# Sums of a normalised input taken from PSUM, tile by tile, in a one-core Trainium2 transformer layer

## The chip, the cores and the metric

The kernel is one program on one core of one Trainium2 chip. The core has a matrix engine (TensorE, called PE in the profile, with its weight loads as PEld), a vector engine (VectorE, DVE), an activation engine (ScalarE, ACT), a general engine (GpSimd, POOL) and a queue that issues the DMA transfers (SyncE, SP). Each engine works through its own list of instructions in order, and waits for the others through semaphores. The metric is the device time of one execution in microseconds (us).

## The reference, cut to what matters

One decoder layer on 1024 tokens of width 1024, in float32. What the change touches is its second half: the residual sum, the second norm, and the feed-forward (FF) block of width 2816.

```python
h = x + merged @ w_out
hn = rms_norm(h, norm_ffn)
return h + (jax.nn.silu(hn @ w_gate) * (hn @ w_up)) @ w_down
```

Every float32 operand is held as a high part (rounded to the matrix engine's type) and a low part (what is left over), and every product is three matmuls: high by high, high by low, low by high.

## The kernel before, in words

**The output projection and the norm.** The 1024 tokens are four tiles of 256 rows, `tp` = 0 to 3. The loop over `c4` computes 256 columns of `h` at a time: `tok_proj` (48 matmuls of 256 columns) for each tile, an add of `x` on VectorE, and the squares on ScalarE. In the last round (`c4` = 3) `norm_h` follows one tile behind. It multiplies the tile's rows by their reciprocal norm and by the gain (`scalar_tensor_tensor`, two of 1024 elements), turns them with 16 transposes into four PSUM banks, and for each bank takes the high half on ScalarE and the low half on VectorE (`split`, 512 elements each) into the operand slabs `XN[half]`. Here `half` is the left or right operand of 512 tokens: tiles 0 and 1 are half 0, tiles 2 and 3 half 1. The program has eight PSUM banks: seven for `bank` in three small pools, one for `fbank`.

**FF blocks the plain way.** FF has 22 blocks of 128 columns. `plain(f, half, w)` is the direct way: 24 matmuls of 512 columns for the gate, 24 for the up projection, `silu` on ScalarE, the product on VectorE. Block 0 is done so after the last output projection, with tile 3's norm between its halves, and so is block 1. One block takes 96 matmuls.

**FF blocks with seven products.** From block 2 on `seven` computes the four products of half by gate or up with the Winograd form of Strassen's scheme: seven products of half the depth, 12 matmuls each, 84 in all. It wants sums of the weights, which `pieces` makes one block ahead (four operations on GpSimd, splits on ScalarE and VectorE), and four sums of the normalised input, `T[0]` to `T[3]`, each in two slabs (`j` = 0, 1). `sums` makes these after the norm from the slabs `XN`, high and low parts apart: `j` = 0 on GpSimd and `j` = 1 on VectorE, ten operations of 1024 elements each, and then splits them. Block 1 stands behind `sums` in program order.

**What sets the order.** The program is written in the order above; a scheduler then places the instructions on each engine by priority and by when their operands and buffers are free. Buffers come from pools that are reused in turn: 16 slabs, 4 of 4 KB per partition (`t4`), 6 of 2 KB (`t2`), 2 of `fz`, 2 staging buffers for weights. A slab that held `h` of a tile can be reused only when that tile has been stored to memory (`hd`), because `h` is wanted again at the end.

Of the kernel before, what the change touches and what calls it, by code (L numbers as in the profile page):

```python
# [8 lines left out]
F32 = mybir.dt.float32  # L9
# [3 lines left out]
OP = mybir.AluOpType  # L13
# [25 lines left out]
def hybrid_layer_kernel(  # L39
# [26 lines left out]
    def nm(s):  # L66
        count[0] += 1
        return f"{s}_{count[0]}"

    def slab(shape, dt=F32R):  # L70
        return slabs.tile([P] + shape, dt, tag="slab", name=nm("slab"))
# [13 lines left out]
    def t4(shape, dt=F32):  # L85
        return t4p.tile([P] + shape, dt, tag="t4", name=nm("t4"))
# [39 lines left out]
    def sub(eng, o, a, b):  # L126
        eng.tensor_tensor(o, a, b, op=OP.subtract)  # L127

    def split(hi, lo, src, eng=None):
        nc.scalar.copy(hi, src)  # L130
        sub(eng or nc.vector, lo, src, hi.bitcast(F32))
# [70 lines left out]
    def transpose_pair(js, dests):  # L202
        for kp in range(4):
            b = bank([2, 256])
            for kk in range(2):
                k = 2 * kp + kk
                for tt in range(2):
                    nc.tensor.transpose(b[:, kk, tt * P:(tt + 1) * P], js[tt][:, k * P:(k + 1) * P], ident)  # L208
            hi, lo = dests(kp)
            split(hi, lo, b)  # L210
# [605 lines left out]
    def left_low(f, a0, a1):  # L816

        s_ = t2([512])
        sub(nc.gpsimd, s_, a0, a1)
        nc.sync.dma_start(ads[2, f], s_)  # L820
# [14 lines left out]
    def gate_up(f):  # L835
        return [col_unit(w, f * P, alloc=anyslab) for w in (w_gate, w_up)]

    def plain(f, half, w):
# [5 lines left out]
        emit_act(f, half, s_)  # L844
        return s_

    def norm_h(tp):
        half, q = tp // 2, tp % 2
        if q == 0:
            for kp in range(4):  # L850
                XN[half][kp] = slab([2, 2, 512])
        ss = small(2)
        nc.vector.tensor_reduce(ss, sq4[tp].rearrange("p (t c) -> p t c", t=2), axis=AX.X, op=OP.add)
        r = recip_rms(ss, D, RMS_EPS, 2)
        js = (t4([D]), t4([D]))
        for tt in range(2):
            nc.vector.scalar_tensor_tensor(js[tt], H[tp][:, tt, :], r[:, tt:tt + 1], gff, op0=OP.mult, op1=OP.mult)
        transpose_pair(js, lambda kp: tuple(XN[half][kp][:, hl, :, q * 256:(q + 1) * 256] for hl in range(2)))

    H = [None] * 4  # L860
    gff = fstp.tile([P, D], F32, tag="fst", name="gff")
# [2 lines left out]
    for c4 in range(4):  # L864
        ws = row_units(w_out, c4 * 256, alloc=anyslab)
        if c4 == 3:
            w0 = gate_up(0)
        for tp in range(4):
            xr = t2([2, 256])
            nc.sync.dma_start(xr, x[tp * 256:(tp + 1) * 256, c4 * 256:(c4 + 1) * 256]  # L870
                              .rearrange("(t p) d -> p t d", p=P))
            if c4 == 0:
                H[tp] = slab([2, D], F32)
            ps = tok_proj(ws, tp, mg, anybank)
            h = H[tp][:, :, c4 * 256:(c4 + 1) * 256]
            nc.vector.tensor_tensor(h, ps, xr, op=OP.add)
            for tt in range(2):
                nc.scalar.activation(xr[:, tt], h[:, tt], AF.Square, accum_out=sq4[tp][:, 4 * tt + c4:4 * tt + c4 + 1])
            if c4 == 3 and tp > 0:
                norm_h(tp - 1)  # L880
    a0 = plain(0, 0, w0)
    norm_h(3)
    left_low(0, a0, plain(0, 1, w0))


    T = [[None] * 2 for _ in range(4)]

    def sums(j, eng):
        def add(o, a_, b_):
            eng.tensor_tensor(o, a_, b_, op=OP.add)  # L890

        (l0, l1), (r0, r1) = [[XN[h_][j + 2 * u][:].bitcast(F32) for u in range(2)] for h_ in range(2)]
        d = []
        for n_ in range(4):
            v = t4([2, 512])
            if n_ in (0, 2):
                p_, q_ = (r0, l0) if n_ == 0 else (r1, r0)
                e = t4([2, 512])
                sub(eng, v, p_[:, 0], q_[:, 0])
                sub(eng, e, p_[:, 1], q_[:, 1])  # L900
                add(v, v, e)
            else:
                p_, q_ = (r1, d[0]) if n_ == 1 else (l1, d[1])
                sub(eng, v, p_[:, 0], q_)
                add(v, v, p_[:, 1])
            d.append(v)
            T[n_][j] = slab([2, 2, 512])
            split(T[n_][j][:, 0], T[n_][j][:, 1], v)

    def pieces(f):  # L910
        st = []
# [59 lines left out]
        emit_act(f, 0, c11)  # L971
        (left_low if f < FH else left_high)(f, c11, u4)

    for tp in range(4):
        nc.sync.dma_start(hd[tp], H[tp])
    sums(0, nc.gpsimd)
    sums(1, nc.vector)
    w1 = gate_up(1)
    left_low(1, plain(1, 0, w1), plain(1, 1, w1))
    w = pieces(2)  # L980
    for f in range(2, FF // P):
        nxt = pieces(f + 1) if f + 1 < FF // P else None
        seven(f, *w)
        w = nxt
# [92 lines left out]

    def into(B, th, dh, final):
        for t in range(4):
            h = H[2 * th + t // 2][:, t % 2, cols[dh]]  # L1080
            nc.vector.tensor_tensor(h, B[t], h, op=OP.add)
            if final:
                r0 = th * 512 + t * P
                nc.sync.dma_start(out[r0:r0 + P, cols[dh]], h)

    product(X, p1, True)
# [42 lines left out]
```

## Time and profile before

| what | value |
|---|---|
| time, median of 3 runs | 1765.89 us (1764.24 to 1766.59) |
| time of the profiled execution | 1765.17 us |
| its span, first to last instruction | 1763.4 us |
| mean granted TensorE clock | 0.991 |
| PE busy | 1706.7 us, 97% of the span |
| DVE, ACT, POOL busy | 1071.1, 724.7, 664.4 us |
| chain that ended last | PE 84%, DVE 10%, POOL 2% of the span |

The chain that ended last is followed back from the last instruction, at each step to what released it. Nearly all of it is PE; where another engine stands in it, PE waited there.

### The profile page before, as it was taken

How to read it: one execution, taken by the hardware profiler on the slowest of the kernel's cores; microseconds unless marked ns; L12 is line 12 of the kernel's file. 1: busy time of each engine (PE TensorE's matmuls, PEld its weight loads, DVE VectorE, ACT ScalarE, POOL GpSimd, SP SyncE). 2: the span in 40 equal slices, each digit the busy share in tenths (PEclk: the TensorE clock that was granted, in tenths of full speed). 3: DMA queues.
4: the chain of work that ended last, by engine and by line, in shares of the span. 5: the costliest groups of instructions: out<-in, count | busy, mean ns of one | idle time of the engine just before them, and what ended most of it. 6: DMA issues, size and time to landing. Idle time of an engine off the chain costs nothing.

```text
span 1763.4 us, 25092 instructions
## 1 busy us (share of the span) xinstructions
PE 1706.7 (97%) x9431; PEld 1482.2 (84%) x9431; DVE 1071.1 (61%) x1794; ACT 724.7 (41%) x1355; POOL 664.4 (38%) x543
## 2 busy tenths in 40 slices
PE   7999779999999999999999999989999999999999
PEld 6887669899988888989888899868888888888887
DVE  5599994435445667767755623596454554457655
ACT  6212224344455666766654423333222222234332
POOL 1113458333343434434203500456656767510000
PEclk9999899999999999999999999989999999999999
DMA  6113314211122111111286323123233444794673
GB/s 220 48 27 114 126 42 132 78 55 39 65 66 64 49 37 49 37 34 46 86 300 202 121 73 120 72 72 120 90 107 117 140 156 157 245 394 166 213 242 124
DMA packets 178527, 204.59 MB, mean 116 GB/s; under 512 B 10788, under 2 KB 125764, under 8 KB 177382
## 3 DMA queue, kind: packets, MB, share of 16 engines
q1 hardware_dynamic: 178406, 202.99, 35.2%
q8 instruction: 74, 1.21, 0.3%
q14 instruction: 47, 0.39, 0.1%
HBM read 152.62 MB, written 50.33 MB: 115 GB/s over the span
## 4 chain that ended last, share of the span: by engine, by line
PE 84%; DVE 10%; POOL 2%; ACT 1%; DMA 1%; issue 1%; SPq 0%; DVEq 0%; ACTq 0%; POOLq 0%
PE ps L141 51%; PE pf L141 16%; PE ps L1064 11%; DVE slab L360 6%; PE ps L714 3%; PE pf L1064 1%; DVE slab L127 1%; POOL wsl L127 1%; DVE t L127 1%; POOL t L127 1%; PE ps L208 1%; DMA slab<-in_x_dram 1%; DMA fst<-in_w_in_dram 0%; PE ps L640 0%; PE ps L515 0%
## 5 line engine op out<-in xcount | busy, mean ns | idle before, releaser
L141 PE MATMUL ps<-slab,wsl 128*128 128x512 f32 x1596 | 370.9, 390 | 0.3 <-ACT wsl L130 0.3
L141 PEld LDWEIGHTS ps<-slab,wsl 128*128 128x128 f32 x1596 | 299.0, 188 | 63.1 <-ACT wsl L130 0.8
L141 PE MATMUL pf<-slab,fsl 128*128 128x512 f32 x1260 | 327.8, 399 | 4.5 <-ACT fz L765 1.8
L141 PEld LDWEIGHTS pf<-slab,fsl 128*128 128x128 f32 x1260 | 226.6, 188 | 46.8 <-ACT fz L765 3.6
L141 PE MATMUL ps<-wsl,slab 128*128 128x256 f32 x1744 | 235.7, 291 | 12.9 <-POOL wsl L127 8.1
L141 PEld LDWEIGHTS ps<-wsl,slab 128*128 128x128 f32 x1744 | 225.3, 198 | 16.7 <-POOL wsl L127 8.5
L360 DVE SCALAR_TENSOR_TENSOR slab<-slab,cw 128x1007 f32<-128x1007 f32 (+27 forms) x120 | 174.5, 1501 | 0.4
L954 DVE TENSOR_TENSOR t<-ps,t 128x512 f32<-128x512 f32 x124 | 85.0, 688 | 109.2 <-PE ps L141 104.4
L127 DVE TENSOR_TENSOR t<-ps,t 128x512 fp32r<-128x512 f32 (+2 forms) x192 | 117.5, 630 | 44.6 <-ACT t L130 43.1
L141 PE MATMUL ps<-slab,fsl 128*128 128x512 f32 x612 | 142.1, 389 | 0.0
L141 PEld LDWEIGHTS ps<-slab,fsl 128*128 128x128 f32 x612 | 114.9, 188 | 23.9
L1064 PE MATMUL ps<-wsl 128*128 128x512 f32 x504 | 120.6, 389 | 0.0
L127 POOL TENSOR_TENSOR wsl<-st,wsl 128x1024 fp32r<-128x1024 f32 x20 | 72.9, 3659 | 122.9 <-ACT wsl L130 110.4
L141 PE MATMUL ps<-t,slab 128*128 128x256 f32 x624 | 115.6, 292 | 2.6 <-DVE t L127 2.1
L130 ACT CAST t<-ps 128x512 fp32r<-128x512 f32 (+2 forms) x192 | 97.9, 540 | 42.1 <-PE ps L714 30.5
L130 ACT CAST wsl<-st 128x1024 fp32r<-128x1024 f32 x66 | 69.3, 1050 | 110.5 <-PE ps L141 66.4
L1064 PEld LDWEIGHTS ps<-wsl 128*128 128x128 f32 x504 | 94.6, 188 | 19.6
L141 PEld LDWEIGHTS ps<-t,slab 128*128 128x128 f32 x624 | 93.9, 189 | 9.5 <-DVE t L127 3.0
L141 PE MATMUL ps<-slab,qt 128*128 128x384 f32 (+3 forms) x384 | 96.2, 342 | 0.5 <-DVE sm L682 0.5
L127 POOL TENSOR_TENSOR fsl<-fst,fsl 128x1024 fp32r<-128x1024 f32 x24 | 62.7, 2614 | 81.2 <-ACT fsl L130 81.2
L127 DVE TENSOR_TENSOR wsl<-st,wsl 128x1024 fp32r<-128x1024 f32 x46 | 62.3, 1355 | 49.9 <-ACT wsl L130 49.8
L628 POOL TENSOR_SCALAR wsl<-wsl,sm 128x640 f32<-128x640 f32 (+7 forms) x76 | 52.7, 707 | 91.2 <-DVE sm L626 53.4
(238 smaller groups left out, 2772.5 us busy)
## 6 DMA issues: line engine op xcount, KB each, us to landing
t<-in_w_down_dram SPq DMA_DIRECT2D x70, 256.0 KB, 3.8
fst<-in_w_in_dram SPq DMA_DIRECT2D x24, 512.0 KB, 3.9
zd<-fz SPq DMA_DIRECT2D x48, 256.0 KB, 2.0
t<-zd SPq DMA_DIRECT2D x24, 512.0 KB, 3.5
st<-in_w_in_dram SPq DMA_DIRECT2D x22, 512.0 KB, 3.9
st<-in_w_gate_dram SPq DMA_DIRECT2D x22, 512.0 KB, 4.0
st<-in_w_up_dram SPq DMA_DIRECT2D x22, 512.0 KB, 4.4
ad<-t SPq DMA_DIRECT2D x44, 256.0 KB, 2.4
```

The lines of the kernel that those rows point to most:

```text
L127: eng.tensor_tensor(o, a, b, op=OP.subtract)
L130: nc.scalar.copy(hi, src)
L141: return nc.tensor.matmul(o, a, b, start=start, stop=stop)
L208: nc.tensor.transpose(b[:, kk, tt * P:(tt + 1) * P], js[tt][:, k * P:(k + 1) * P], ident)
L360: nc.vector.scalar_tensor_tensor(acc[:, s:], u[:, :S - s], cw[:, ct, 30 - s:31 - s], acc[:, s:], op0=OP.mult, op1=OP.add)
L628: nc.gpsimd.tensor_scalar(tiles[h], tiles[h], c[:, h:h + 1], 1.0, op0=OP.mult, op1=OP.mult)
L714: nc.tensor.transpose(b[:, j - j0, h, :], tiles[h][:, j * P:(j + 1) * P], ident)
L954: nc.vector.tensor_tensor(o, a_, b_, op=OP.add)
L1064: nc.tensor.matmul(B[t], a_, b_, start=start and k == 0 and j == 0, stop=k == FH - 1 and j == 2, skip_group_check=True)
```

## The change

Tiles 0 and 2 are now half 0 and tiles 1 and 3 half 1, so that a pair of tiles (0 and 1, then 2 and 3) gives 256 columns of both halves. `norm_h` of an even tile copies the four turned banks, besides splitting them, to SBUF (`raw`). `norm_h` of an odd tile subtracts: its own banks in PSUM against `raw` give the sums for those 256 columns, eight operations of 512 elements on VectorE, and `keep` splits each of them into its half of the slab `T[n][j]`. Of the first pair, the splits of `T[1]` and `T[2]` are put off until the last output projection has been written, those of `T[3]` until the second pair. The function `sums` is gone, with its twenty operations of 1024 elements, GpSimd's ten among them. Block 1 is done by `seven`, and `pieces(1)` takes the place of `gate_up(1)`. The stores of `h` are issued per tile. The rows of the output are addressed by the new halves.

```diff
     def norm_h(tp):
-        half, q = tp // 2, tp % 2
+        half, q = tp % 2, tp // 2
+        c = slice(q * 256, (q + 1) * 256)
...
-        transpose_pair(js, lambda kp: tuple(XN[half][kp][:, hl, :, q * 256:(q + 1) * 256] for hl in range(2)))
+        def turned(kp):
+            b = bank([2, 256])
+            for kk in range(2):
+                k = 2 * kp + kk
+                for tt in range(2):
+                    nc.tensor.transpose(b[:, kk, tt * P:(tt + 1) * P], js[tt][:, k * P:(k + 1) * P], ident)
+            split(XN[half][kp][:, 0, :, c], XN[half][kp][:, 1, :, c], b)
+            return b
+
+        def keep(n, j, v, c=c):
+            if T[n][j] is None:
+                T[n][j] = slab([2, 2, 512])
+            split(T[n][j][:, 0, :, c], T[n][j][:, 1, :, c], v)
+
+        if half == 0:
+            raw[0], raw[1] = [sb_fz() for _ in range(2)], t4([2, 2, 256])
+            for kp in range(4):
+                nc.scalar.copy(raw[0][kp] if kp < 2 else raw[1][:, kp - 2], turned(kp))
+            return
+        for j in range(2):
+            r0, r1 = turned(j), turned(j + 2)
+            l0, l1 = raw[0][j], raw[1][:, j]
+            d0, d1, d2 = (t2([2, 256]) for _ in range(3))
+            sub(nc.vector, d0, r0, l0)
+            keep(0, j, d0)
+            sub(nc.vector, d1, r1, d0)
+            sub(nc.vector, d2, d1, l0)
+            sub(nc.vector, l1, l1, d1)
+            later = [lambda n=n, j=j, v=v: keep(n, j, v) for n, v in ((1, d1), (2, d2))]
+            held[0] += later
+            held[1].append(lambda j=j, v=l1: keep(3, j, v))
+            if q == 1:
+                for f_ in held[0] + held[1][j::2]:
+                    f_()
+                held[0].clear()
...
-            if c4 == 3 and tp > 0:
-                norm_h(tp - 1)
+            if c4 == 3:
+                nc.sync.dma_start(hd[tp], H[tp])
+                if tp == 3:
+                    for f_ in held[0]:
+                        f_()
+                    held[0].clear()
+                if tp > 0:
+                    norm_h(tp - 1)
...
-    sums(0, nc.gpsimd)
-    sums(1, nc.vector)
-    w1 = gate_up(1)
-    left_low(1, plain(1, 0, w1), plain(1, 1, w1))
-    w = pieces(2)
-    for f in range(2, FF // P):
+    w = pieces(1)
+    for f in range(1, FF // P):
```

**VectorE around the add of tile 3.** This is VectorE's list around the last add of the output projection, which writes tile 3's columns into `slab_10303`; before, with the end of tile 2's norm ahead of it and the start of tile 3's norm (`TENSOR_REDUCE`) behind it:

```order
L857 SCALAR_TENSOR_TENSOR t_1885_11134<-slab_10248,sm_11132,gff 128x1024
L857 SCALAR_TENSOR_TENSOR t_1886_11135<-slab_10248,sm_11132,gff 128x1024
L127 TENSOR_TENSOR wsl_11382<-st_11380,wsl_11382 128x1024
L876 TENSOR_TENSOR slab_10303<-ps_11072,t_1876_11070 128x2x256
L853 TENSOR_REDUCE sm_11220<-sm_10125 128x2
```

Now, where `slab_10938` to `slab_10940` are the low halves of tile 2 and the other slabs ahead of the add are parts of `T`:

```order
L127 TENSOR_TENSOR slab_10938<-ps_11184,slab_10938 128x2x256
L127 TENSOR_TENSOR slab_10939<-ps_11192,slab_10939 128x2x256
L127 TENSOR_TENSOR slab_10940<-ps_11200,slab_10940 128x2x256
L127 TENSOR_TENSOR t_1888_11095<-ps_11087,t_1887_11094 128x512
L127 TENSOR_TENSOR slab_11098<-t_1887_11094,slab_11098 128x2x256
L127 TENSOR_TENSOR slab_11159<-t_1882_11071,slab_11159 128x2x256
L127 TENSOR_TENSOR slab_11162<-t_1883_11072,slab_11162 128x2x256
L127 TENSOR_TENSOR t_1889_11096<-t_1888_11095,fz_10953 128x512
L127 TENSOR_TENSOR t_1863_10954<-t_1863_10954,t_1888_11095 128x512
L127 TENSOR_TENSOR slab_11165<-t_1888_11095,slab_11165 128x2x256
L920 TENSOR_TENSOR slab_10303<-ps_11106,t_1891_11104 128x2x256
```

Between tile 2's second `SCALAR_TENSOR_TENSOR` and tile 3's add there was one operation; now there are 18 of 512 elements, the ten shown ahead of the add and eight ahead of those.

**ScalarE around its change of tables.** ScalarE's list from the square root of tile 3's norm (line 135) to the high halves of its turned banks; before (the rows on `slab_11124` to `slab_11127` ahead of the table load are tile 2's):

```order
L135 ACTIVATE sm_11222<-sm_11220 128x2
L130 CAST slab_11124<-ps_11138 128x2x256
L130 CAST slab_11125<-ps_11145 128x2x256
L130 CAST slab_11126<-ps_11152 128x2x256
L130 CAST slab_11127<-ps_11159 128x2x256
L130 CAST u_1945_11509<-st_11498 128x512
L841 ACT_TABLE_LOAD
L841 ACTIVATE t_1892_11191<-ps_11166 128x512
L130 CAST slab_11124<-ps_11230 128x2x256
```

Now (`slab_11339` is the second slab of `T[3]`, its first 256 columns):

```order
L135 ACTIVATE sm_11272<-sm_11270 128x2
L885 COPY t_1904_11183<-ps_11208 128x512
L130 CAST slab_11339<-t_1863_10954 128x2x256
L841 ACT_TABLE_LOAD
L841 ACTIVATE t_1910_11241<-ps_11216 128x512
L130 CAST slab_11042<-ps_11280 128x2x256
```

The table load for `silu` of block 0 (line 841) now stands behind a part of `T[3]`. `slab_11339` is the slab that held tile 3's `h`, so this cast waits for tile 3's norm and for its store.

**TensorE behind tile 3's norm.** TensorE's list from the third of tile 3's four banks (`ps_11319`) to the first matmuls of the second half of block 0; now:

```order
L873 MATMUL ps_11319<-ident,t_1916_11277 128x128
L873 MATMUL ps_11287<-ident,t_1915_11276 128x128
L873 MATMUL ps_11287<-ident,t_1916_11277 128x128
L873 MATMUL ps_11287<-ident,t_1915_11276 128x128
L873 MATMUL ps_11287<-ident,t_1916_11277 128x128
L141 MATMUL ps_11344<-slab_11042,wsl_10820 128x512
```

The order of these is as it was before. New is what the fourth bank, `ps_11287`, waits for: it takes the buffer of `ps_11243`, the up product of block 0's first half, so it waits until VectorE's product of line 843 has read that. Before, all four waited for the norm alone.

## Rows read from the trace of the kernel before

**Rows 1.** Chain that ended last, in order of time: start us, us, engine, line.

```profile
1167.46 3.03 DVE t L890 x2
...
1210.27 19.04 PE ps L141 x84
```

**Rows 2.** Busy time by stretch: us, then PE, PEld, DVE, ACT, POOL (instructions), PEclk, DMA share, GB/s.

```profile
1160.00:1170.00 10.00, 4.79 (x22) 3.62 (x20) 10.00 (x10) 2.17 (x3) 3.01 (x2) 0.88 0.07 26
1170.00:1180.00 10.00, 6.85 (x18) 4.40 (x19) 9.55 (x7) 5.25 (x6) 7.11 (x4) 0.61 0.39 121
```

**Rows 3.** PE's timeline from 1103 us: start us, us, operation xcount [idle before <-releaser].

```profile
1103.17 1.91 PE L208 MATMUL ps<-ident,t 128*128 128x128 f32 x16
1104.83 1.67 PE L141 MATMUL ps<-wsl,slab 128*128 128x256 f32 x12
...
1110.66 2.01 PE L141 MATMUL ps<-slab,wsl 128*128 128x512 f32 x8
...
1125.09 0.71 PE L141 MATMUL ps<-slab,wsl 128*128 128x512 f32 x2
...
1163.26 1.52 PE L141 MATMUL pf<-slab,u 128*128 128x512 f32 x6
1172.72 0.80 PE L141 MATMUL pf<-slab,u 128*128 128x512 f32 x1 [7.94 <-ACT slab L130]
1173.80 2.08 PE L141 MATMUL ps<-slab,wsl 128*128 128x512 f32 x4 [0.28 <-ACT wsl L130]
1176.02 2.24 PE L141 MATMUL pf<-slab,u 128*128 128x512 f32 x5
```

**Rows 4.** DVE's timeline from 1103 us, with the same columns.

```profile
1103.37 0.69 DVE L876 TENSOR_TENSOR slab<-pf,t 128x512 f32<-128x512 f32 x1 [0.21 <-PE pf L141]
...
1111.65 0.69 DVE L876 TENSOR_TENSOR slab<-ps,t 128x512 f32<-128x512 f32 x1
...
1113.99 2.48 DVE L857 SCALAR_TENSOR_TENSOR t<-slab,sm,gff 128x1024 f32<-128x1024 f32 x2
1116.39 2.48 DVE L127 TENSOR_TENSOR slab<-ps,slab 128x512 fp32r<-128x512 f32 x4
1118.78 0.69 DVE L127 TENSOR_TENSOR u<-st,u 128x512 fp32r<-128x512 f32 x1
...
1181.87 1.30 DVE L127 TENSOR_TENSOR u<-st,u 128x512 fp32r<-128x512 f32 x1 [0.18 <-ACT u L130]
```

**Rows 5.** ACT's timeline, with the same columns.

```profile
1091.81 1.28 ACT L135 ACT_TABLE_LOAD   x1
1093.11 0.20 ACT L135 ACTIVATE sm<-sm 128x2 f32<-128x2 f32 x1
...
1115.10 2.06 ACT L130 CAST slab<-ps 128x512 fp32r<-128x512 f32 x4 [1.34 <-PE ps L208]
1117.02 0.66 ACT L130 CAST u<-st 128x512 fp32r<-128x512 f32 x1
1117.69 1.28 ACT L841 ACT_TABLE_LOAD   x1
1119.99 0.60 ACT L841 ACTIVATE t<-ps 128x512 f32<-128x512 f32 x1 [1.01 <-PE ps L141]
```

**Rows 6.** POOL's timeline, with the same columns.

```profile
1168.21 2.25 POOL L127 TENSOR_TENSOR t<-t,t 128x512 f32<-128x512 f32 x1
```

**Rows 7.** The stores to hd (line 975): times from issue to landing.

```profile
DMA to landing us min/median/max: 3.9/4.0/4.5
```

**Rows 8.** The loads from hd (line 1023), near the end: the same.

```profile
DMA to landing us min/median/max: 12.4/12.4/12.4
```

**Rows 9.** Two gaps of PE, earlier: its timeline, and stretches as in rows 2.

```profile
240.79 2.18 PE L141 MATMUL ps<-wsl,slab 128*128 128x256 f32 x16 [2.21 <-DVE slab L127]
240.00:242.00 2.00, 1.21 (x10) 1.22 (x11) 2.00 (x4) 0.41 (x1) 0.00 (x0) 1.00 0.00 0
1175.00:1177.50 2.50, 2.35 (x7) 1.34 (x6) 2.50 (x2) 0.38 (x2) 2.11 (x1) 0.50 0.47 137
```

More of the change, by code (lines that the diff above doesn't have):

```diff
@@ L845, in plain, with sb_fz @@
         return s_
+    T = [[None] * 2 for _ in range(4)]
+    raw, held = [None, None], [[], []]
+    def sb_fz():
+        return fzp.tile([P, 2, 256], F32, tag="fz", name=nm("fz"))
     def norm_h(tp):
-        half, q = tp // 2, tp % 2
+        half, q = tp % 2, tp // 2
+        c = slice(q * 256, (q + 1) * 256)
         if q == 0:
@@ L883, in hybrid_layer_kernel @@
     left_low(0, a0, plain(0, 1, w0))
[L886 to L908, printed above, removed]
     def pieces(f):
@@ L972, in seven @@
         (left_low if f < FH else left_high)(f, c11, u4)
-    for tp in range(4):
-        nc.sync.dma_start(hd[tp], H[tp])
-    sums(0, nc.gpsimd)
-    sums(1, nc.vector)
-    w1 = gate_up(1)
-    left_low(1, plain(1, 0, w1), plain(1, 1, w1))
-    w = pieces(2)
-    for f in range(2, FF // P):
+    w = pieces(1)
+    for f in range(1, FF // P):
         nxt = pieces(f + 1) if f + 1 < FF // P else None
@@ L1079, in into @@
         for t in range(4):
-            h = H[2 * th + t // 2][:, t % 2, cols[dh]]
+            tp = 2 * (t // 2) + th
+            h = H[tp][:, t % 2, cols[dh]]
             nc.vector.tensor_tensor(h, B[t], h, op=OP.add)
             if final:
-                r0 = th * 512 + t * P
+                r0 = tp * 256 + t % 2 * P
                 nc.sync.dma_start(out[r0:r0 + P, cols[dh]], h)
```

## The prediction, made before the changed kernel ran

> **What bounds the kernel now.** The chain of waits comes first: it is PE for most of the span, and DVE stands in it only where PE waits for a sum or a norm. In the steady FF blocks 84 matmuls take 19.04 us [rows 1], so one of 512 columns costs 0.227 us at the full clock and twelve cost 2.72. That is one `seven` block. Then the table by stretches, to find where PE is not busy in the second half: from 1160 to 1180 us it is busy 11.6 of 20, and the granted clock falls to 0.88 and 0.61 [rows 2]. PE's timeline there shows the wait: the last matmul ends at 1164.8, the next starts 7.94 us later behind ScalarE's copy of a slab, and until 1178.2 only 1 + 4 + 5 = 10 run [rows 3], at half clock, 0.50 in 1175 to 1177.5 [rows 9]. In these 13.4 us PE did 10 x 0.227 = 2.3 us of work, so **the stall costs 11.1 us**. It ends with the sums of `j` = 1, which VectorE makes on the chain [rows 1]. From 1110.66 to the stall PE is without a gap [rows 3].
>
> **What the change removes.** (a) Block 1 costs 84 matmuls, not 96: -2.7 us. (b) `sums` goes, and with it the stall of 11.1, if its work is done in time elsewhere. The most that can be gained is 13.8.
>
> **What it adds, and where it lies.** PE has no more transposes, 64 as before. VectorE gets 16 subtractions and 16 low halves of 512 elements, ScalarE 16 high halves and 8 copies. A VectorE operation of 512 elements takes 0.69 alone and 0.60 in a row: four take 2.48 [rows 4]. ScalarE takes 0.66 for a cast from SBUF, and 2.06 for four from PSUM [rows 5]. What matters is what waits behind them. I walk the lists.
>
> Tile 2. PE ends its projection as before at 1103.2, and VectorE's add stood at 1103.37 [rows 4]. Four low halves of tile 0 are moved ahead, so I put the add at 1103.7. From add to scaling, tile 3 shows 1113.99 - 1111.65 = 2.34 [rows 4]: the scaling starts at 1106.05. One scaling is 1.20 of the pair's 2.48.
>
> Tile 1's banks. PE does 4 transposes, 23 small matmuls and 12 transposes. Sixteen transposes take 1104.83 - 1103.17 = 1.66, and tile 3's 48 small matmuls 1110.66 - 1104.83 = 5.83 [rows 3], 0.12 each. The first bank is full near 1107.0, its high half is copied by 1107.6. From there VectorE runs: low half and first difference (1.2), second scaling of tile 2 (1.2), eight of 512 elements (4.8). So the low half of tile 2's first bank starts at 1114.8 and ends at **1115.5**. PE ends tile 3's projection at 1110.7 and twelve transposes at 1111.9, and block 0's first half, which began at 1110.66 [rows 3], now needs that low half. PE can do two matmuls in between and loses 3.1 us.
>
> Tile 3. Ten more operations (6.0) stand ahead of its add: it starts at **1120.8, not 1111.65**. Add to the end of scaling: 2.34 + 2.48, and 0.9 more, since a ScalarE copy now stands between squares and root and a low half between root and reciprocal: 1126.5. PE, from 1115.5, does the 46 matmuls left and four transposes in 10.9, to 1126.4: level.
>
> Then comes the fourth bank of tile 3. It waits for the product of line 843, that for `silu`, `silu` for the table load, and the load stands behind a part of `T[3]` that waits for the scaling (1126.5) and for the store of tile 3's `h`. Cast 0.66, load 1.28, `silu` 0.60 [rows 5], product 0.69 and 0.1 of hand-offs: 3.3, so 1129.8, and four transposes: 1130.2. The second half of block 0 starts there, and before it started at 1125.09 [rows 3]. **The norm costs PE 5.1 us more.** The first loss is inside these 5.1: the second half's start is set by VectorE and ScalarE, not by PE.
>
> One rule is weighed here. The row shows 1.28 for the load of a table and the next activation 0.02 behind it (1091.81 and 1093.11) [rows 5]. The Trainium skill, "ScalarE: Activation LUTs", section "What ACT_TABLE_LOAD costs", gives about 1283 ns and a drain of about 1380 ns for every switch. By that the path would be 1.4 longer and the time 1758.7; I take the row.
>
> The store: `hd` lands 3.9 to 4.5 after issue [rows 7]. Issued at 1121.6, it lands by 1126.1, 0.4 ahead of the scaling. It costs nothing, with little to spare.
>
> From 1130.2 PE has block 0's second half (48) and two products of block 1 that need no sum (24): 16.3, to 1146.5; the last part of `T[1]` is wanted 11 matmuls later, at 1149.0. VectorE has, after 1129.8, 21 operations up to that part: 18 of 512 (10.8) and 3 of 1024 (3.6 at twice that), so 1144.2 if nothing is late. GpSimd starts the weight sums of block 1 only near 1128, when a `t4` buffer of `raw` is free, and takes 2.25 for each of four while VectorE works [rows 6], to 1137. The next gate weights take that staging buffer; at 4 us as for the stores [rows 7] they land at 1141.4, are cast, and VectorE's split of them, ahead of the last five operations, ends at 1144: with those 1147. Hidden, with 2 us to spare, so I cost `T` at nothing. The eight raw copies lie on ScalarE beside tile 3's projection and cost nothing beyond the 0.9. Moving the `hd` stores ahead of tile 3's load of `x` delays that load, which is wanted only at 1120.8.
>
> **The sum.** -11.1 - 2.7 + 5.1 = -8.7. Against the profiled execution's 1765.17: 1756.5. The median of the runs lies 0.7 above that execution, so **1757.2**.
>
> **Bounds.** If VectorE's chain hides fully, the 5.1 goes: 1752.1. If its some 25 operations on the path take 0.69 instead of 0.60 and each of a dozen hand-offs costs 0.1: +3.4, 1760.6. I take the pitch, since such groups ran at it [rows 4].
>
> **Rivals.**
>
> *The clock falls again.* PE waits 3.1 us near 1113 and 2 us near 1128. For it: the gap of 7.94 brought 0.50, and PE ran at that from 1172.7 to past 1177.5 [rows 3, 9], some 5 us of half speed, 2.5 lost. Against it: a gap of 2.21 at 240 left 1.00 [rows 9]. A fall in the first wait is mostly covered by the second; one in the second costs 2.5: 1759.7.
>
> *The sums come late after all.* A VectorE split of 512 with both inputs in SBUF took 1.30 instead of 0.69 when GpSimd worked beside it [rows 4]. If the ten such among the 18 pay 0.6 and three of 1024 pay 1.2, `T[1]` ends 9.6 later, of which 1149.0 - 1144.2 = 4.8 are hidden: +4.8, 1762. Against: GpSimd has only four operations, 9 us, in that stretch, so half of it is likely, which is hidden. The Trainium skill, "SBUF — State Buffer", section "Who interferes with whom", says that such a pair excludes each other for the whole instruction, and that a VectorE operation with one SBUF input is free of it. By that four GpSimd operations of 1.28 block VectorE by at most 5.1.
>
> *Slower: the store of tile 3.* ScalarE's cast waits for it, and behind it stand the table load, `silu`, and all high halves of tile 3. The loads from `hd` took 12.4 [rows 8]. At that the cast starts at 1134, 7.5 later, and PE's wait is then long enough to lose 2.5 at half clock, as 7.94 was: 1767.2, slower than before. It decides from a landing of some 11 us on. Against: all four stores took at most 4.5 [rows 7], and nothing else is in the queue then.
>
> *The stall only moves.* If PE waits at block 1's first sum as long as it did in the stall, what is left is -2.7 + 5.1 = +2.4: 1768.3, slower as well. Against: the weights of block 1 are asked for where `gate_up(1)`'s were, and the 16.3 us of work ahead of that sum cover GpSimd's 9 and the splits.
>
> **Chances.** The forecast with its own range 1755 to 1759.5: 50%. Less norm cost, 1752 to 1755: 10%. Clock: 13%. Longer chain or late sums, 1759.5 to 1763: 17%. The stall moves: 5%. Store: 5%. What a measurement of this kernel can tell from no change is about 0.2%, 3.5 us: 1762.4 to 1769.4. Faster 0.87, same 0.08, slower 0.05. The range 1752.5 to 1762.5 leaves out some 2 in 10.
>
> **What would show it.** In the profile after: tile 3's add (line 920) near 1121, a PE gap of some 3 us near 1113, a second of 2 us ahead of four late transposes, the table load near 1127, the second half of block 0 at 1130, no gap from there to the last product, the clock 1.00 throughout. Wrong would be: a gap at a `T` product, a clock of 0.5 between 1112 and 1150, ScalarE waiting for a DMA ahead of the table load, or gaps in the FF blocks or in the last stage, where block 1's fewer buffer turns shift which pool each operand takes.

## The result, and the profile after

The changed kernel takes 1754.86 us, the median of 6 runs (1754.19 to 1758.84); the kernel before took 1766.04 beside it (6 runs, 1763.95 to 1766.60). The ratio is 0.9944, with a 95% interval of 0.9931 to 0.9957 (it is one of means, which are 9.9 us apart): faster by 11.2 us between the medians, where the forecast was faster by 8.7. The profiled execution has a span of 1753.4 us, 10.0 less than before. The runs of one kernel often lie in two groups (of the thirteen of the kernel before that were taken beside the last experiment on the store, six are at 1763.8 to 1764.6 us, one at 1765.3, six at 1766.5 to 1767.2), so a difference of medians can hold a share of that distance.

**One point to count from.** Up to the end of tile 2's output projection TensorE's list is the same in both programs, and yet TensorE is there at 1101.87 us now and was there at 1103.17 [rows 3]. These 1.30 us are no part of the forecast; they are taken up at the end. From that point to the end of the span it is 660.2 us before and 651.5 now: **-8.7**. All times of the profile after stand 1.30 below those of the prediction, and are given with the 1.30 added where they are compared.

TensorE's timeline, the answer to [rows 3] (start us, us, operation xcount, idle before and what ended it):

```profile
1101.87 0.60 PE L873 MATMUL ps<-ident,t 128*128 128x128 f32 x4
...
1110.87 0.50 PE L141 MATMUL ps<-slab,wsl 128*128 128x512 f32 x1
1113.63 7.44 PE L141 MATMUL ps<-slab,wsl 128*128 128x512 f32 x23 [2.27 <-DVE t L127]
1120.91 0.60 PE L873 MATMUL ps<-ident,t 128*128 128x128 f32 x4
1121.27 5.74 PE L141 MATMUL ps<-slab,wsl 128*128 128x512 f32 x24
1126.85 1.47 PE L873 MATMUL ps<-ident,t 128*128 128x128 f32 x12
1128.84 0.66 PE L873 MATMUL ps<-ident,t 128*128 128x128 f32 x4 [0.52 <-DVE t L843]
1129.25 0.70 PE L141 MATMUL ps<-slab,wsl 128*128 128x512 f32 x2
```

The stall of 7.94 us is gone: behind 1129.25 no matmul waits. Two waits are new, 2.27 us behind the first matmul of block 0's gate and 0.52 us ahead of tile 3's fourth bank. The 23 matmuls behind the first took 7.44 us, not 23 x 0.227 = 5.2. The table by stretches says why (us, then PE, PEld, DVE, ACT, POOL, granted clock, DMA):

```profile
1114.00:1120.00 6.00, 5.96 (x20) 4.63 (x19) 6.00 (x11) 4.34 (x9) 0.00 (x0) 0.72 0.00 0
1120.00:1126.00 6.00, 6.00 (x30) 4.96 (x29) 4.60 (x8) 2.66 (x8) 0.00 (x0) 1.00 0.42 175
```

The granted clock averaged 0.72 of 2.4 GHz in the first stretch, so TensorE ran part of it at 1.2 GHz, after its idle 2.27 us. VectorE worked without a gap in it, and on what, its timeline shows; this answers to [rows 4]:

```profile
1102.30 0.68 DVE L920 TENSOR_TENSOR slab<-pf,t 128x512 f32<-128x512 f32 x1
...
1112.81 0.68 DVE L127 TENSOR_TENSOR t<-ps,fz 128x512 f32<-128x512 f32 x1
1113.41 1.87 DVE L127 TENSOR_TENSOR slab<-ps,slab 128x512 fp32r<-128x512 f32 x3
...
1119.41 0.68 DVE L920 TENSOR_TENSOR slab<-ps,t 128x512 f32<-128x512 f32 x1
...
1122.96 2.48 DVE L866 SCALAR_TENSOR_TENSOR t<-slab,sm,gff 128x1024 f32<-128x1024 f32 x2
1126.18 0.69 DVE L127 TENSOR_TENSOR slab<-t,slab 128x512 fp32r<-128x512 f32 x1 [0.73 <-ACT slab L130]
1128.09 0.69 DVE L843 TENSOR_TENSOR t<-ps,t 128x512 f32<-128x512 f32 x1 [1.22 <-ACT t L841]
```

What ended the 2.27 us is the row at 1112.81, not a low half: the releaser writes `t`, and a low half writes a `slab`. It is the first difference of the slabs `j` = 1, and it is the last to read one of tile 1's PSUM banks. The second matmul in TensorE's list is the first of block 0's up product, and the up product takes that bank. The first low half of tile 2 stands right behind on VectorE (the first of the three at 1113.41), and the third matmul needs it, so without the wait for the bank TensorE would have come no further.

ScalarE's timeline, which answers to [rows 5]:

```profile
1125.52 0.62 ACT L130 CAST slab<-t 128x512 fp32r<-128x512 f32 x1 [2.04 <-DVE t L866]
1126.16 1.28 ACT L841 ACT_TABLE_LOAD   x1
1127.46 0.60 ACT L841 ACTIVATE t<-ps 128x512 f32<-128x512 f32 x1
```

The cast into tile 3's slab was released by the scaling, not by the store; the table load and `silu` stand right behind it.

### The profile page after: what moved, and what is told of

Read it like the earlier page. It is cut to its first block, busy times and chain, and to the rows that moved or that the text cites. A ratio compares the mean times of both kernels' runs of the same rounds, so it can differ in the third digit from the quotient of the medians.

```text
span 1753.4 us, 25116 instructions
## 1 busy us (share of the span) xinstructions
PE 1706.2 (97%) x9419; PEld 1482.5 (85%) x9419; DVE 1067.9 (61%) x1815; ACT 731.4 (42%) x1374; POOL 637.1 (36%) x539
## 4 chain that ended last, share of the span: by engine, by line
PE 84%; DVE 9%; POOL 2%; ACT 2%; issue 1%; DMA 1%; SPq 0%; DVEq 0%; ACTq 0%; POOLq 0%
PE ps L141 52%; PE pf L141 16%; PE ps L1084 11%; DVE slab L360 7%; PE ps L714 3%; PE pf L1084 1%; POOL wsl L127 1%; DMA slab<-in_x_dram 1%; DMA fst<-in_w_in_dram 0%; DVE t L127 0%; PE ps L640 0%; DVE slab L127 0%; PE ps L515 0%; POOL fsl L127 0%; PE ps L698 0%
## 5 line engine op out<-in xcount | busy, mean ns | idle before, releaser
L141 PE MATMUL ps<-slab,wsl 128*128 128x512 f32 x1536 | 357.8, 391 | 2.3 <-DVE t L127 2.3
L141 PEld LDWEIGHTS ps<-slab,wsl 128*128 128x128 f32 x1536 | 288.6, 188 | 63.2 <-issue 2.6
L141 PE MATMUL pf<-slab,fsl 128*128 128x512 f32 x1236 | 322.8, 399 | 4.3 <-ACT fz L765 1.8
L141 PEld LDWEIGHTS pf<-slab,fsl 128*128 128x128 f32 x1236 | 222.6, 189 | 45.7 <-ACT fz L765 3.6
L360 DVE SCALAR_TENSOR_TENSOR slab<-slab,cw 128x1007 f32<-128x1007 f32 (+27 forms) x120 | 182.8, 1570 | 0.4
L141 PE MATMUL ps<-slab,fsl 128*128 128x512 f32 x636 | 147.8, 389 | 0.0
L127 DVE TENSOR_TENSOR t<-ps,t 128x512 fp32r<-128x512 f32 (+3 forms) x196 | 120.2, 630 | 45.1 <-ACT t L130 43.5
L141 PEld LDWEIGHTS ps<-slab,fsl 128*128 128x128 f32 x636 | 119.4, 188 | 24.8
L127 POOL TENSOR_TENSOR wsl<-st,wsl 128x1024 fp32r<-128x1024 f32 x20 | 63.6, 3196 | 124.9 <-ACT wsl L130 111.4
L127 DVE TENSOR_TENSOR wsl<-st,wsl 128x1024 fp32r<-128x1024 f32 x45 | 58.7, 1305 | 45.2 <-ACT wsl L130 44.8
```

The source lines that it names most:

```text
L141: return nc.tensor.matmul(o, a, b, start=start, stop=stop)
L360: nc.vector.scalar_tensor_tensor(acc[:, s:], u[:, :S - s], cw[:, ct, 30 - s:31 - s], acc[:, s:], op0=OP.mult, op1=OP.add)
```

## The experiments

Eleven runs. In each the time is compared with the kernel before on the same chip; the column "rest" is the span less the moment at which TensorE ends tile 2's projection, worked out from each profile as 1753.4 - 1101.87 = 651.5 for the changed kernel. It leaves out what the stages ahead of the norm did in that one execution.

| run | median us (runs) | ratio to before, 95% interval | end of tile 2's projection | rest |
|---|---|---|---|---|
| before | 1766.04 (6) | | 1103.17 | 660.2 |
| before, two more profiles | 1765.75, 1766.08 (1 each) | | 1103.77, 1104.10 | 660.2, 660.3 |
| changed | 1754.86 (6) | 0.9944, 0.9931 to 0.9957 | 1101.87 | 651.5 |
| changed, again | 1755.14 (5) | 0.9945, 0.9931 to 0.9959 | 1102.03 | 651.0 |
| block 1 plain | 1758.73 (5) | 0.9963, 0.9951 to 0.9976 | 1101.49 | 654.7 |
| late sums | 1786.41 (4) | 1.0118, 1.0104 to 1.0132 | 1105.22 | 681.4 |
| layout only | 1766.03 (11) | 1.0000, 0.9991 to 1.0009 | 1104.20 | 660.4 |
| lows first | 1759.30 (5) | 0.9964, 0.9951 to 0.9978 | 1104.29 | 653.0 |
| tile 3 early | 1757.83 (5) | 0.9950, 0.9937 to 0.9963 | 1101.80 | 650.6 |
| both | 1754.32 (5) | 0.9932, 0.9919 to 0.9945 | 1101.74 | 648.7 |
| store late | 1757.95 (5) | 0.9953, 0.9940 to 0.9966 | 1105.03 | 651.2 |
| store late, order held | 1764.99 (10) | 0.9998, 0.9988 to 1.0007 | 1101.79 | 660.4 |

### Which part of the change gains: three runs

**Block 1 plain again, sums in the norm.**

```diff
-    w = pieces(1)
-    for f in range(1, FF // P):
+    w1 = gate_up(1)
+    left_low(1, plain(1, 0, w1), plain(1, 1, w1))
+    w = pieces(2)
+    for f in range(2, FF // P):
```

> The changed kernel with FF block 1 done the plain way again; the sums stay in the norm. If the gain is the stall plus twelve matmuls of 0.227 us, this costs the twelve back and nothing else: 2.7 us over the changed kernel's 1754.9, so 1757.6, with no gap of TensorE between the norm and the last stage. The rival, that the stall was in truth one of block 2's weights and only moved out of sight, gives a gap of TensorE in block 2 and 1760 or more.

Measured: 3.2 us more in the rest than the first profile of the changed kernel, 3.7 more than the second (both in the table), 3.9 by the medians, and no wait of TensorE behind the norm. The twelve matmuls are 2.7 of it. In the norm TensorE waited 0.7 longer than in the first profile: 2.27 + 1.18 for 2.27 + 0.52. The 1.18 is for the first low half of tile 2, ahead of which VectorE now made a split of block 1's weights:

```profile
1113.26 0.47 PE L141 MATMUL ps<-slab,wsl 128*128 128x512 f32 x1 [2.27 <-DVE t L127]
1114.90 6.92 PE L141 MATMUL ps<-slab,wsl 128*128 128x512 f32 x22 [1.18 <-DVE slab L127]
```

The stall did not come back, in block 2 or elsewhere, although the weights of block 1 and the sums of block 2's are made here as in the kernel before. So it is the early sums of the input that take the stall away.

**Late sums: the kernel before with block 1 by `seven`.**

```diff
-    w1 = gate_up(1)
-    left_low(1, plain(1, 0, w1), plain(1, 1, w1))
-    w = pieces(2)
-    for f in range(2, FF // P):
+    w = pieces(1)
+    for f in range(1, FF // P):
```

> The kernel before, with its sums made in a step of their own behind the norm, but with FF block 1 done with seven products. If the stall waits for the sums, TensorE now meets it one block of 84 matmuls (19.04 us) earlier, while the sums end at about the same time, 1172 us or some us sooner because block 1's plain weights are no longer split ahead of them: 1766 + 19 = 1785, or 1778 to 1785. The rival, that TensorE waited for block 2's weights and not for the sums, gives 2.7 less than before: 1763.

Measured: 1786.4, a little above the 1778 to 1785 expected: 20 us slower than before, the rest 21.1 longer. Its TensorE timeline and the end of GpSimd's:

```profile
1141.29 2.43 PE L141 MATMUL ps<-slab,fsl 128*128 128x512 f32 x10
1176.17 1.22 PE L141 MATMUL pf<-slab,fsl 128*128 128x512 f32 x2 [32.45 <-ACT fsl L130]
```

```profile
1152.42 3.20 POOL L890 TENSOR_TENSOR t<-t,slab 128x1024 f32<-128x1024 f32 x1
...
1167.37 3.26 POOL L919 TENSOR_TENSOR t<-st 128x512 f32<-128x512 f32 x1 [11.75 <-DVE t L127]
...
1175.12 1.27 POOL L127 TENSOR_TENSOR t<-st,t 128x512 f32<-128x512 f32 x1
```

The wait grew from 7.94 to 32.45 us, and the last thing in it was the sums of block 1's *weights*: GpSimd made them only after its share of the old `sums`, when VectorE had let go of a buffer. So seven products in block 1 without early sums lose far more than 2.7 us: this edit needs the other, while the sums gain without it (block 1 plain). How much of the 32.45 us the sums of the input would have cost by themselves, with the weights in time, this run does not show.

**Layout only: the kernel before with alternate tiles as halves.**

```diff
-        half, q = tp // 2, tp % 2
+        half, q = tp % 2, tp // 2
...
-            h = H[2 * th + t // 2][:, t % 2, cols[dh]]
+            tp = 2 * (t // 2) + th
+            h = H[tp][:, t % 2, cols[dh]]
...
-                r0 = th * 512 + t * P
+                r0 = tp * 256 + t % 2 * P
```

> The kernel before, with the token halves made of alternate tiles and nothing else: sums in a step of their own, FF block 1 plain. If the 5 us that the norm costs TensorE come from VectorE's and ScalarE's work on the sums, the layout alone costs little: 1766 to 1768, the second half of block 0 within 2 us of 1125.09, and the stall of 8 us is still there. The rival, that waiting for tile 2 instead of tile 1 is what costs the 5 us, gives 1771 and a start of that half near 1130.

Measured: no difference, and the stall is there. TensorE's timeline of this run:

```profile
1113.36 11.39 PE L141 MATMUL ps<-slab,wsl 128*128 128x512 f32 x48
1124.59 1.91 PE L208 MATMUL ps<-ident,t 128*128 128x128 f32 x16
1126.25 0.71 PE L141 MATMUL ps<-slab,wsl 128*128 128x512 f32 x2
...
1173.88 0.80 PE L141 MATMUL pf<-slab,u 128*128 128x512 f32 x1 [7.92 <-ACT slab L130]
```

The second half of block 0 starts 22.05 us after tile 2's projection, as before (21.92, from 1103.17 and 1125.09 [rows 3]); in the changed kernel it is 27.38. The 5 us that the norm costs come from the work on the sums, not from the halves.

### Where the norm's 5 us are set: three runs

In these three, VectorE's and ScalarE's order is set by hand, through a dependence that carries no wait; `lows`, `more`, `scaled`, `flushed`, `cast`, `highs` hold the instructions of the low halves, of the operations on the sums, of the scalings, and so on.

**Lows first: tile 2's low halves ahead of four operations on the sums; all else as it was.**

```diff
+    for kp in range(3):
+        for i_ in more[1, 0]:
+            behind(i_, lows[2, kp])
+    behind(silu[0, 0], cast[3, 1, 0])
```

> The changed kernel with VectorE's three low halves of tile 2 ahead of four operations on the sums of tiles 0 and 1, so that TensorE's first wait (2.27 us near 1111, and the half clock behind it) goes; the work ahead of tile 3's add and the chain of the table load are as they were. The theory of the prediction says that VectorE and ScalarE set the start of block 0's second half: it stays at 1129 and the time at 1754.9, or up to 2.2 us more, because the waits that are left are now some 5 us in one piece and may bring the half clock later. The rival, that the first wait is itself the loss, gives 4.5 less: 1750.4.

Measured: 1.5 to 2.0 us slower in the rest than the two profiles of the changed kernel, 4.4 by the medians. TensorE's timeline, and two rows by stretch:

```profile
1114.15 8.23 PE L141 MATMUL ps<-slab,wsl 128*128 128x512 f32 x35 [0.37 <-DVE slab L882]
1122.23 0.60 PE L879 MATMUL ps<-ident,t 128*128 128x128 f32 x4
1123.50 0.73 PE L141 MATMUL ps<-slab,wsl 128*128 128x512 f32 x2 [0.67 <-ACT slab L881]
1124.54 2.57 PE L141 MATMUL ps<-slab,wsl 128*128 128x512 f32 x10 [0.31 <-DVE slab L882]
...
1127.98 1.20 PE L879 MATMUL ps<-ident,t 128*128 128x128 f32 x9 [0.54 <-DVE t L871]
1131.06 1.20 PE L141 MATMUL ps<-slab,wsl 128*128 128x512 f32 x2 [1.88 <-ACT slab L881]
```

```profile
1116.00:1118.00 2.00, 2.00 (x11) 1.65 (x10) 1.97 (x4) 0.86 (x2) 0.00 (x0) 1.00 0.39 119
...
1132.00:1134.00 2.00, 2.00 (x6) 1.54 (x5) 2.00 (x4) 1.51 (x2) 0.20 (x1) 0.50 0.34 131
```

The first wait fell from 2.27 to 0.37 us (the scheduler also put the up product behind the gate's first matmuls, so its bank was not waited for), the clock stayed full behind it, and nothing was gained: TensorE came earlier to the next operand, waited 0.67 + 0.31 + 0.54 + 1.88 there, and the half clock came behind the last of these, where no wait covers it. In the rest this is what the theory gave (0 to +2.2) and not the rival's -4.5. The 4.4 between the medians lie outside what was expected. This one profile was at the common point 2.42 us later than the changed kernel's first; the other runs have no trace.

**Tile 3 early: its add and scaling moved up, operations on the sums put behind them, the T casts behind `silu`.**

```diff
+            if (c4, tp) == (3, 3):
+                xr = stage.tile([P, 2, 2, 256], F32, tag="st", name=nm("st"))[:, 0]
...
+    behind(added, lows[2, 2])
+    for i_ in more[1, 0] + [dif[1, 1, 0]]:
+        behind(lows[2, 0], i_)
+    for i_ in more[1, 1] + flushed:
+        behind(i_, scaled[3])
+        behind(i_, lows[2, 3])
+    for i_ in (cast[3, 1, 0], cast[3, 0, 0], cast[2, 1, 0]):
+        behind(i_, highs[3, 2])
+    behind(flushed[3], lows[3, 2])
```

> The changed kernel with tile 3's add and scaling some 5 us earlier on VectorE (its x goes into a staging buffer; nine operations on the sums of tiles 0 and 1 stand behind its scaling) and with the casts of those sums behind silu and tile 3's high halves on ScalarE; the low halves of tile 2, for which TensorE waits near 1111, stay where they are. TensorE's second wait was 0.52 us, so the theory gives at most 0.9 us: 1754.0 to 1754.9 by the median, and 650.6 to 651.5 from the end of tile 2's projection to the end of the span, where the changed kernel has 651.5. The rival, that the chain behind tile 3's add is all of the 5 us that the norm costs, gives 4.5 to 5 less: 1750.

Measured: 0.4 to 0.9 less in the rest (650.6) than the two profiles of the changed kernel, as the theory gave, not 4.5 to 5. The first wait was still there, ended by the same difference of VectorE (line 901 in this kernel):

```profile
1114.36 5.80 PE L141 MATMUL ps<-slab,wsl 128*128 128x512 f32 x23 [2.51 <-DVE t L901]
```

The second was gone. Two small ones are new: 0.38 us for tile 1's scaling and 0.30 at a split of block 1's weights. The median of 1757.83 is above the changed kernel's, although the rest is shorter; the five runs spread from 1754.2 to 1758.8, and the profile is of the fastest. The median alone would have misled, and the rest is that of one execution.

**Both edits.** The lines of tile 3 early, with the first loop replaced by

```diff
+    for i_ in more[1, 0]:
+        behind(i_, added)
```

> The changed kernel with both orders: tile 2's three low halves ahead of the operations on the sums of tiles 0 and 1, and tile 3's add right behind them. By the theory two equal losses cover each other, so that either edit alone gains under 1 us and the two together most of the 5: the second half of block 0 starts some 4 us earlier after tile 2's projection, 647 to 648 us from there to the end of the span instead of 651.5, and 1750 to 1751.5 by the median; the clock stays at 1.00. The rival: the operations put off make the sums of tiles 2 and 3 late, TensorE waits at a product with T in block 1, and 2 to 4 us are given back: 1752 to 1755.

Measured: 648.7 in the rest, 2.3 to 2.8 less than the two profiles of the changed kernel, where 4 were expected. The edits apart gave +1.5 and -0.9 against the first of them. TensorE's timeline of this run:

```profile
1102.37 0.63 PE L879 MATMUL ps<-ident,t 128*128 128x128 f32 x4 [0.47 <-DVE t L871]
...
1112.50 4.15 PE L141 MATMUL ps<-slab,wsl 128*128 128x512 f32 x17 [0.61 <-DVE slab L882]
1116.49 0.60 PE L879 MATMUL ps<-ident,t 128*128 128x128 f32 x4
1116.85 7.10 PE L141 MATMUL ps<-slab,wsl 128*128 128x512 f32 x30
1123.78 1.47 PE L879 MATMUL ps<-ident,t 128*128 128x128 f32 x12
1125.80 0.72 PE L141 MATMUL ps<-slab,wsl 128*128 128x512 f32 x2 [0.54 <-ACT slab L881]
```

Three waits of 0.47, 0.61 and 0.54 are left, one of them new: with another order on VectorE tile 1's scaling came later. No product with T waited, so the rival fell, and the clock was 1.00 throughout. The median of 1754.32 lies in the rival's 1752 to 1755 and above the 1750 to 1751.5 expected, but the rival's mechanism did not occur. By its median this version is ahead of the kernel before beside it (1765.56) by 11.2 us and of the changed one by 0.5 to 0.8, which these runs can't tell from nothing; by the rest of one profile each it is the fastest of all.

### The store of tile 3: two runs

**Store late: the store made three times over.**

```diff
-                nc.sync.dma_start(hd[tp], H[tp])
+                for _ in range(3 if tp == 3 else 1):
+                    nc.sync.dma_start(hd[tp], H[tp])
```

> The changed kernel with tile 3's h stored three times over, so that the last of the three lands some 6 to 8 us later. By the rival of the prediction on this store, ScalarE's cast into that slab, the table load and silu wait for it: the cast starts near 1131 instead of 1125.5, the second half of block 0 some 5 to 7 us later, and half a clock's worth of 2 us may follow: 1760 to 1764. If the cast does not really wait for the store, nothing changes: 1754.9.

Measured: nothing changed in the rest (651.2). The median of 1757.95 is 3.1 us above the changed kernel's, and the common point of this profile is 3.2 later. But the experiment did not try what it was meant to: with the longer store the scheduler put the cast into that slab behind `silu`. ScalarE's timeline of this run:

```profile
1129.08 1.28 ACT L841 ACT_TABLE_LOAD   x1 [2.47 <-PE ps L141]
1130.37 0.60 ACT L841 ACTIVATE t<-ps 128x512 f32<-128x512 f32 x1
```

It shows something else. The cast was off the path, and the second half of block 0 still started 1132.16 - 1105.03 = 27.13 us after the common point, against 27.38 and, in the second profile of the changed kernel, 26.79. The table load began only when TensorE's gate product was there, though ScalarE had been idle for 2.47 us: in ScalarE's list of this run a separate wait for that product stands ahead of the load, where in the changed kernel `silu` itself has the wait.

**The same with ScalarE's order held.**

```diff
+    behind(silu[0, 0], cast[3, 1, 0])
+    for kp in (0, 1, 3):
+        behind(highs[3, kp], silu[0, 0])
```

> Tile 3's h stored three times over as before, but now with ScalarE's order held: the cast into that slab stays ahead of the table load and silu, and the casts of tile 3's first three banks stay behind silu. The three stores go one behind the other, so the last lands some 13 us after the first is issued. By the prediction's rival on this store the cast then starts some 7.5 us later than in the changed kernel, the second half of block 0 with it, and a wait of that length may cost up to 2.5 us at half clock: 659 to 661.5 us from the end of tile 2's projection to the end of the span (the changed kernel: 651.5), and 1762 to 1765. If the store were no wait of that cast, nothing would change.

Measured: 660.4 in the rest and 1764.99, all of the gain gone. ScalarE, TensorE and the stretches:

```profile
1132.26 0.62 ACT L888 CAST slab<-t 128x512 fp32r<-128x512 f32 x1 [9.38 <-DMA hd<-slab]
1132.90 1.28 ACT L841 ACT_TABLE_LOAD   x1
```

```profile
1135.32 1.22 PE L141 MATMUL ps<-slab,wsl 128*128 128x512 f32 x2 [7.60 <-ACT slab L880]
```

```profile
1136.00:1138.00 2.00, 2.00 (x6) 1.57 (x5) 2.00 (x5) 1.50 (x3) 0.45 (x1) 0.50 0.34 131
1138.00:1140.00 2.00, 2.00 (x6) 1.56 (x5) 1.64 (x2) 0.31 (x1) 0.00 (x0) 0.50 0.00 0
```

The cast waited for the store and started 6.7 us later than in the changed kernel (1132.26 against 1125.52, at nearly the same common point), TensorE lost 7.60 in one wait, and the half clock followed it. The sum is +8.9, where the prediction's rival had 7.5 + 2.5.

### The stages ahead of the norm: three runs

The changed kernel unaltered, and the kernel before twice, for more profiles.

> The changed kernel once more, unaltered. The profiled execution reached the end of tile 2's projection 1.30 us earlier than the one before, though the program up to there is the same. If that is chance between executions, this profile shows that point anywhere within 2.5 us of 1103 and again 651.5 +- 0.5 us from there to the end, and the median lies at 1754.5 to 1757. If the change itself made the stages ahead of the norm quicker, the point is at 1101.9 again and the median at 1754.9.

> The kernel before, unaltered, for a second profile. If the 1.30 us by which the changed kernel's profiled execution was ahead at the end of tile 2's projection are chance, that point lies anywhere from 1101.5 to 1105.5 in profiles of the same kernel; if they belong to the kernel, it is at 1103.2 +- 0.3 again. From there to the end of the span: 660.2 +- 0.5.

> The kernel before, unaltered, for a third profile; the same two expectations: the end of tile 2's projection anywhere from 1101.5 to 1105.5 if it is chance, 1103.2 +- 0.3 if it belongs to the kernel, and 660.2 +- 0.5 from there to the end.

Measured: the rests agree within 0.6 us for the changed kernel and 0.1 for the kernel before, so the -8.7 to -9.3 behind the common point are firm. The point itself was at 1103.17, 1103.77 and 1104.10 in the kernel before, two of them outside 1103.2 +- 0.3, where it was expected if the kernel sets it, and at 1101.87 and 1102.03 in the changed one. The instructions up to there do not set it: lows first and store late have the changed kernel's list on every engine up to that point, and were there at 1104.29 and 1105.03. Where the profiles part is told in the last section.

In the second profile of the changed kernel the same first wait left the clock at 1.00. Its TensorE timeline:

```profile
1113.79 5.79 PE L141 MATMUL ps<-slab,wsl 128*128 128x512 f32 x23 [2.26 <-DVE t L127]
...
1128.41 0.66 PE L873 MATMUL ps<-ident,t 128*128 128x128 f32 x4 [1.59 <-DVE t L843]
```

TensorE saved the 1.65 us of the half clock and gave 1.07 of them back in the second wait, 1.59 instead of 0.52.

## Why the prediction was right, step by step

**The sum.** It said -11.1 - 2.7 + 5.1 = -8.7. From the start of block 0's second half to the end, the span fell from 638.3 to 624.15: -14.2, where -13.8 was forecast for the stall and the twelve matmuls; with 2.72 for the matmuls the stall comes to 11.5, for 11.1. The norm cost 27.38 - 21.92 = 5.5 in the first profile and 4.9 in the second, for 5.1. That the first profile gives -8.7 to the tenth is luck in part, since +0.4 and -0.4 cancel; the second gives -9.3. Block 1 plain shows the term of the twelve matmuls (3.2 to 3.9 with longer waits in the norm) and that the stall goes with the early sums alone; layout only shows that the new halves do nothing. The sum that gives 1758.7 with the drain should give 1757.2 + 1.4 = 1758.6, and nothing hangs on it.

**The walk through the lists.** Forecast, and measured with the 1.30 added:

| step | forecast | measured |
|---|---|---|
| tile 2's add | 1103.7 | 1103.60 |
| first low half of tile 2 starts | 1114.8 | 1114.71 |
| tile 3's add | 1120.8 | 1120.71 |
| tile 3's scaling ends | 1126.5 | 1126.74 |
| table load starts | 1127.2 | 1127.46 |
| product of line 843 ends | 1129.8 | 1130.08 |
| block 0's second half starts | 1130.2 | 1130.55 |

Counting the operations ahead of an instruction at the pitch of such operations placed a chain of some 40 instructions on three engines within 0.4 us. The second part of `T[1]` was ready at 1142.99 (1144.29 with the 1.30; forecast 1144.2 to 1147), and no product with T waited.

**Sizes that were off.** TensorE's first wait was 2.27, not 3.1, and its second 0.52 or 1.59, not 2. The first had another cause as well: the forecast let TensorE do two matmuls and then wait for tile 2's low half, and it did one and then waited for a PSUM bank, which the forecast had not counted. It made no difference to the time, because the low half came right behind. The step behind it, "the second half's start is set by VectorE and ScalarE, not by PE", held: lows first took the first wait away and gained nothing. It held by little in the first profile, in which TensorE at half clock was only 0.52 us ahead.

**The rivals.** *The clock falls again* did happen in the first wait of one profile out of two, which is one of the signs that the prediction named for being wrong, and cost what the prediction said of that case: mostly covered by the second wait (0.6 us between the two profiles). The row brought against it, a gap of 2.21 that left 1.00 [rows 9], was no evidence: in the changed kernel's profile the clock is 0.50 from 242 to 244 us behind the same gap, there 2.19. *The sums late* did not occur. *The store of tile 3* did not occur but is real: with the order held it takes the whole gain. In the changed kernel tile 3's store was issued at 1120.12 us, and the stores to `hd` landed 3.9 to 4.7 us after issue, so by 1124.8, 0.6 ahead of the scaling's end at 1125.44. *The stall only moves* fell with block 1 plain and with the profile after. *Less norm cost* (1752 to 1755) holds the measured median of 1754.86, which lies just below the forecast's own 1755 to 1759.5; but the norm did not cost less, and what brought the median there lies ahead of it.

**The rule that was weighed.** The row of this profile has 1.28 us for the table load and the next activation 0.02 us behind its end. The Trainium skill, "ScalarE: Activation LUTs", section "What ACT_TABLE_LOAD costs", adds a drain of about 1.38 us to each switch; no run here shows it.

**What the forecast missed** is the rest of the measured gain: 1.3 of the 10.0 between the profiles, which lies in stages that the change doesn't touch, and about 2.5 of the 11.2 between the medians (1.2 of the 9.9 between the means). Where the runs without a trace have theirs is not shown.

## What to carry to other kernels

Walk each engine's list with the pitch of its operations from the trace, and count what stands ahead: it is accurate to tenths of a microsecond here. When two engines reach a point within a microsecond of each other, an edit on one of them gains little or loses, as the two edits did here (+1.5 and -0.9 in the rest, -2.8 together); move both or neither. When a row names a releaser, read also what it writes: here `t` instead of `slab` told a buffer that came free from an operand that came late. Compare profiles from a common point behind which the programs differ, since what one execution does ahead of it can be as large as the effect.

## What the runs showed of the hardware that was not expected

**A half clock that goes with a shorter time.** Near 241 us (245 in late sums) TensorE waits 2.2 us in all thirteen profiles. In the kernel before (three profiles), layout only, lows first and store late the 16 matmuls behind the wait ran at full clock; in the other seven profiles at half clock for a part. Then this follows, on GpSimd in the kernel before,

```profile
250.65 17.18 POOL L127 TENSOR_TENSOR wsl<-st,wsl 128x1024 fp32r<-128x1024 f32 x2 [12.17 <-ACT wsl L130]
```

and on GpSimd and on VectorE in the changed kernel:

```profile
252.32 6.63 POOL L127 TENSOR_TENSOR wsl<-st,wsl 128x1024 fp32r<-128x1024 f32 x2 [13.70 <-ACT wsl L130]
```

```profile
253.93 6.08 DVE L360 SCALAR_TENSOR_TENSOR slab<-slab,cw 128x1002 f32<-128x1002 f32 x2
```

TensorE was late by the half clock, GpSimd's pair of operations started 1.7 us later, and then it took 6.63 us instead of 17.18, while VectorE's two operations beside it took 6.08 (2.41 in the kernel before). TensorE had waited 8.11 us for that pair in the kernel before, 1.33 and 2.59 at other places in the changed one. So at one time GpSimd's pair alone was long, and at the other both pairs were. The Trainium skill, "SBUF — State Buffer", section "Who interferes with whom", says that issue order decides which of the two engines blocks. These rows do not show it: GpSimd's pair starts ahead of VectorE's two both times (250.65 and 252.32, against 253.79 and 253.93). All six profiles with the full clock show the long pair and the wait of some 8.1 us behind it, and all seven others the short pair and the short waits. Why the clock fell at 241 us in some and not in others stays open. It does not follow from the instructions up to there: late sums, with the list of TensorE of the kernel before, was on the side of the half clock, and lows first and store late, with the lists of the changed kernel, on the side of the full one. Each kernel was on one side in all of its profiles, but none has more than three.

**Where a table load stands in the list.** In the kernel before, the load for `silu` was done 1.0 us before the operand came [rows 5]. In store late, and in the run with both edits, a separate wait for TensorE's product stands ahead of the load in ScalarE's list. There it began only when the product was there, with ScalarE idle for 2.47 us in store late, so that its 1.28 us lay behind the product and not beside it. This is the order that the scheduler made, and says nothing of the load itself.

**The same wait, either clock.** A wait of 2.27 us in the norm was followed by 1.2 GHz in one execution of the changed kernel, and a wait of 2.26 by 2.4 GHz in another.
